# Two-layer state-space and attention trunk: norm chain in three stages, weights' low parts on VectorE, tables behind h, gate row on the load queue

## The chip, the cores and the metric

One core of one Trainium2 chip runs the whole program. The metric is device time in microseconds (us), the median over runs; lower is better. Engine names below are those of the profile: PE is TensorE (PEld its weight loads), DVE VectorE, ACT ScalarE, POOL GpSimd, SP the queue from which nearly all loads are issued.

## The reference, cut to what matters

Two layers (`DEPTH = 2`) over 512 tokens of width 1024, all in float32. Each layer is a mixer and a feed-forward part, each between two RMS norms:

```python
mod = silu(c) @ w_ada[l] + b_ada[l]          # six vectors of 1024: shift, scale, gate for both parts
h = rmsnorm(x, g_pre_mix) * (1 + scale_m) + shift_m
u, q, k, v, f_logit, g_a, g_b = split(h @ w_in)
y_ssm = s5_branch(u, ...)                    # state-space scan per group, then a GLU
y_att = forgetting_attention(q, k, v, f_logit, b_f)
merged = sigmoid(g_a) * (y_ssm @ w_pa) + sigmoid(g_b) * (y_att @ w_pb)
x = x + gate_m * rmsnorm(merged @ w_o, g_post_mix)
h = rmsnorm(x, g_pre_ffn) * (1 + scale_f) + shift_f
y = (silu(h @ w_ffn_gate) * (h @ w_ffn_up)) @ w_ffn_down
x = x + gate_f * rmsnorm(y, g_post_ffn)
```

## The kernel before, in words

**Products in three parts.** A float32 matrix is split into a high part (fp32r, made by an ACT cast, L235) and a low part (the difference, made by a subtraction, L236). Each product is three matmuls on PE: high by high, high by low, low by high. `unit` (L228) loads 512 KB of a weight into a `wraw` buffer from the SP queue (a ring of three, shared with the `aw` loads of the modulation), casts it and subtracts. Pairs go to a ring of three (`wpair`) or to buffers that are kept (`khi`/`klo`, `kept`). Which engine subtracts is told by strings at the end of `trunk`: `LO_F` (first gate and up weights of the FFN), `LO_O` (the output projection), `LO_Q` (the q and k weights of layer 1); "g" is POOL and "v" DVE. All other units use DVE, but for the four first `w_u` units, which use POOL.

**Order of the work.** PE runs in program order. The other engines' queues are ordered by a list scheduler that follows program order and a priority (`high_priority(offset=300)` lifts an instruction). `Weave` counts PE's time in `W.t` from matmul sizes; `run` walks over a list of jobs, prepares loads some 11 us ahead, and between groups of matmuls polls side generators, each of which says with `yield t` after how much PE time it wants to go on. So a `yield` decides where in PE's order, and in program order, the next piece of a side job stands.

**Side generators that matter here.**

- `ada_later` (L197): the modulation vectors `mod`, 512 columns ("half") at a time: four loads `aw`, eight DVE steps over 128x512 into `acc` (L210, L212), matmuls `adap` that sum over partitions, a transpose, `derive`. For layer 0's third to fifth vector with pace 4.0, for the last seven, in layer 0's FFN, with pace 3.6.
- `finish` (L371): after the last row of a half (256 tokens) of a part's output: factors of the output norm (a chain of eleven small DVE steps, L308 and L285 to L301), the new x (L368), its squares on ACT (L386), the factors again, the scaled copy on ACT (L390); then after `WAIT["m"]` four times four transposes `hT` on PE, and `split_h` (L327), which makes high and low part of h (ACT L336, DVE L337 and L338).
- `gate_row` (L316): the row `grow` by which the output is multiplied (L364): a DMA from POOL's queue writes 1024 single values of `modg` to DRAM (L320), a second one reads them back to all partitions (L321).
- `ssm_consts` (L572): tables and matrices of the state-space branch for a quarter of the groups: B, T on POOL, G partly on DVE; PE turns B (`bltp`) and forms `mtp`. Layer 0's are made in its mixer, layer 1's ahead, in layer 0's FFN (`ssm_ahead`, L661), and stored in DRAM.
- `ssm_small` (L483): some two hundred DVE steps over 128x32 at the start, of which `ssm_consts` is built.
- `forget` (L815): the decay of the attention; its matmuls `fp`, then ACT and DVE steps in turn.

**Around the parts.** After the mixer's output projection (`wop`), the FFN's first jobs (`pair_first`, `kept_one`) take h half by half: `gtp` and `upp` into four PSUM buffers, `sil` (L1127) frees `gtp`'s. After the FFN's last products (`dnp`) the next layer's `first4` takes q and k from weights that are kept.

Of the kernel before, what the change touches and what calls it, by code (L numbers as in the profile page):

```python
# [11 lines left out]
F32 = mybir.dt.float32  # L12
# [65 lines left out]
def trunk(tc, a, out, dbg=None):  # L78
# [13 lines left out]
    with contextlib.ExitStack() as ctx:  # L92
# [65 lines left out]

        have = set()

        def derive(l, m, c0, c1):
            sl = mod[:, l, 8 * m + c0:8 * m + c1]

            def gv(at):
                return vec[:, l, at + c0:at + c1]
            if m == 1:
                v.scalar_tensor_tensor(modg[:, l, 0, c0:c1], sl, 1.0, gv(VG1), ALU.add, ALU.mult)
            elif m == 4:
                v.scalar_tensor_tensor(modg[:, l, 2, c0:c1], sl, 1.0, gv(VG3), ALU.add, ALU.mult)
# [27 lines left out]
        def ada_later(ns, pace):  # L197

            for n in ns:
                l, m = divmod(n, 6)  # L200
                for hf in range(2):
                    acc = sp.tile([128, 512], F32, tag="acc", name="acc", bufs=1)
                    for q in range(4):
                        w = wp.tile([128, 1024], F32, tag="wraw", name="aw", bufs=3)
                        nc.sync.dma_start(w, a["w_ada"][n - 2, hf, q])
                        for i in range(2):
                            kt = 2 * q + i
                            wk = w[:, 512 * i:512 * i + 512]
                            if kt == 0:
                                v.tensor_scalar(acc, wk, cond[:, 0:1], None, ALU.mult)  # L210
                            else:
                                v.scalar_tensor_tensor(acc, wk, cond[:, kt:kt + 1], acc, ALU.mult, ALU.add)  # L212
                        yield pace if q < 3 else pace + 2.0
                    p = aps("adap")
# [11 lines left out]


        def unit(src, n=1024, at=None, lo_eng=None, pin=False):  # L228
            raw = wp.tile([128, 1024], F32, tag="wraw", name="wraw", bufs=3)
            nc.sync.dma_start(raw[:, 0:n], src)  # L230
            if at is None:
                w = wp.tile([128, 2, 1024], F32R, tag="wpair", name="wpair", bufs=3)
                at = w[:, 0], w[:, 1]
            hi, lo = (x[:, 0:n] for x in at)
            i = sc.copy(hi, raw[:, 0:n])  # L235
            j = (lo_eng or v).tensor_tensor(lo, raw[:, 0:n], hi.bitcast(F32), ALU.subtract)  # L236
            if pin:
                tc.keep_in_program_order(i)
                tc.keep_in_program_order(j)
            return hi, lo  # L240
# [74 lines left out]

        def gate_row(l, which):  # L316

            gi = 1 if which == 0 else 3
            at = tc.dram_tile([KT, 128], F32, name=f"grow{l}{which}")
            g.dma_start(at.rearrange("k p -> p k"), modg[:, l, gi])  # L320
            g.dma_start(grow, at.rearrange("k p -> (k p)").unsqueeze(0).to_broadcast([128, D]))  # L321

# [48 lines left out]
        def finish(l, which, o, hf, nxt):  # L371
# [8 lines left out]
            with tc.high_priority(offset=300):  # L380
                r = factors(o["s"][hf], 2, 2)
                s2 = sums(2)
                ys = []
                for t in range(2):
                    xs, y = new_x(o, hf, t, r[:, t:t + 1])
                    sc.activation(y, xs, AF.Square, accum_out=s2[:, t:t + 1])  # L386
                r = factors(s2, 2)
                for t in range(2):
                    xs, y = xR[:, 2 * hf + t], o["y"][hf][:, t]
                    sc.activation(y, xs, AF.Copy, scale=r[:, t:t + 1])  # L390
                    ys.append(y)
            yield WAIT["m"][which]
            while not o["free"]:
# [178 lines left out]
        def ssm_consts(l, q):  # L572
# [44 lines left out]
            G = quad([128, 2, 4, 4, 2, 16], name="G")  # L617
            g.memset(G, 0.0)
            pmul(v, cf, lpw, lpn, 3, G[:, 0], G[:, 1], 1)
# [5 lines left out]
            T = quad([128, 2, 4, 128], name="T")  # L625
            g.tensor_copy(T[:, :, :, 0:8], head[:, :, ps4])
            for k in range(4):
                rotate(g, T, [phs[k][i][:, ps4] for i in range(2)], 8 << k, 4)
            yield WAIT["b"][l]
# [12 lines left out]
            M = quad([128, 2, 4, 128], name="M")  # L642
            g.memset(M[:, 0], 0.0)
            p = mps("mtp")
# [10 lines left out]
            sc.copy(M[:, 1], rho4[:, ps4].unsqueeze(2).to_broadcast([128, 4, 128]))  # L655
            g.memset(M[:, 1, :, 0:1], 0.0)
            return (blt, G, T, M), (B.rearrange("p i a b c d -> p i (a b c d)"), C.rearrange("p (i a) -> p i a", i=2))
# [157 lines left out]
        def forget(l, st, fw):  # L815
# [142 lines left out]
        def mix_jobs(l, R, st, done, nxt):  # L958

            def f_job(at):  # L960
                if at == FP[l]:
                    job(3.5, 0, lambda: f_weights(l), lambda fw: forget(l, st, fw))

# [107 lines left out]
            def wo_rows(ws, hf, kts, first=False, last=False):  # L1071

                if first and hf == 0:
                    W.wait(lambda: (l, 2) in have)
                    gate_row(l, 0)
                if first:
# [13 lines left out]
                if last:  # L1090
                    W.add(finish(l, 0, o, hf, nxt), 0.0)

# [17 lines left out]
        def ffn_jobs(l, R, prev, nxt):  # L1110
# [133 lines left out]
            def down(w, ts, dh, i, first, last):  # L1244
                if (dh, first) == (0, True):
                    W.wait(lambda: (l, 5) in have)
                    gate_row(l, 1)
                if first:
# [9 lines left out]
                if last and dh:  # L1258
                    W.add(finish(l, 1, d, ts[0] // 2, nxt), 0.0)

# [15 lines left out]
        def first_jobs(l, R, prev, st):  # L1276
# [31 lines left out]
            for hf in range(2):  # L1308
# [64 lines left out]
        for _ in range(4):  # L1373
            next(smalls, None)
        u_done(st, R, pu)
# [108 lines left out]
```

## Time and profile before

| | |
|---|---|
| median of 3 runs | 1606.41 us (1606.28 to 1606.72) |
| profiled execution | 1615.16 us |
| its span in the profile | 1613.4 us |
| PE busy | 1499.9 us (93%) |
| DVE, ACT, POOL busy | 926.4, 622.9, 342.6 us |
| mean granted PE clock | 0.962 of full speed |
| bytes read from HBM | 193.15 MB |

A row of a timeline has the start in us, the duration in us, the engine, the line of the kernel, the operation, output <- inputs by the program's names, and the count of instructions merged; in brackets stand the engine's idle time before it and what ended it. The granted clock is a share of PE's full 2.4 GHz; 0.5 is its lower level of 1.2 GHz.

### The profile page before, as it was taken

To read this page: it belongs to the slowest core of one execution; us is meant where nothing else is said; L and a number is where in the kernel's file an instruction comes from. 1 tells how busy PE (TensorE), PEld (TensorE's weight loads), DVE (VectorE), ACT (ScalarE), POOL (GpSimd) and SP (SyncE) were. 2 spreads that over 40 slices of the span, in tenths; PEclk is the share of its full clock that TensorE was granted. 3 is DMA by queue.
4 is the path that set the end of the run, shared out by engine and by line. 5 is a ranking of instruction groups with operands and counts; after the bars stand their busy time and mean duration, and the time that the engine had idled before them with its cause. 6 is when DMAs were issued, how large, how long until landed. Compare 5 with 4: busy or idle time off the path is not lost.

```text
span 1613.4 us, 21312 instructions
## 1 busy us (share of the span) xinstructions
PE 1499.9 (93%) x8080; PEld 1250.6 (78%) x8080; DVE 926.4 (57%) x1772; ACT 622.9 (39%) x1103; POOL 342.6 (21%) x460
## 2 busy tenths in 40 slices
PE   7799798999879978999996999999997999999997
PEld 6688676778779756878875998877776988888886
DVE  7828866767745776756567249364656322333344
ACT  3235545554432424323235224465534322332231
POOL 1607714332205664000013000032213000000000
PEclk8899899899989989999998999999997999999999
DMA  8221244554203656776664224232332122322341
GB/s 330 62 90 44 79 135 145 182 170 144 80 26 118 207 185 236 227 185 213 209 170 144 105 81 155 92 105 79 105 105 91 32 74 92 101 95 92 104 144 52
DMA packets 57718, 205.06 MB, mean 127 GB/s; under 512 B 7040, under 2 KB 8192, under 8 KB 56592
## 3 DMA queue, kind: packets, MB, share of 16 engines
q1 hardware_dynamic: 54320, 192.16, 36.8%
q0 software_dynamic: 3008, 10.50, 1.8%
q8 instruction: 63, 1.03, 0.3%
q10 hardware_dynamic: 288, 1.05, 0.2%
q14 instruction: 39, 0.32, 0.1%
HBM read 193.15 MB, written 10.53 MB: 126 GB/s over the span
## 4 chain that ended last, share of the span: by engine, by line
PE 62%; DVE 18%; DMA 9%; ACT 4%; POOL 4%; issue 3%; SPq 0%; ACTq 0%; DVEq 0%; POOLq 0%
PE gtp L85 13%; PE upp L85 13%; PE dnp L85 9%; PE gbp L85 5%; PE qkp L85 5%; PE tokp L85 4%; PE gap L85 3%; DVE wpair L236 3%; DMA aw<-in_w_ada_dram 2%; PE pap L85 2%; DMA wraw<-in_w_down_dram 2%; DMA C<-in_bc_dram 2%; DMA wraw<-in_w_up_dram 1%; PE sps L85 1%; PE ops L85 1%
## 5 line engine op out<-in xcount | busy, mean ns | idle before, releaser
L236 DVE TENSOR_TENSOR wpair<-wraw,wpair 128x1024 fp32r<-128x1024 f32 x188 | 235.9, 1256 | 328.6 <-ACT wpair L235 328.2
L235 ACT CAST wpair<-wraw 128x1024 fp32r<-128x1024 f32 x193 | 201.9, 1047 | 339.2 <-issue 88.0
L85 PE MATMUL gtp<-h,wpair 128*128 128x512 f32 (+1 forms) x912 | 210.3, 387 | 21.0 <-ACT sil L1127 21.0
L85 PE MATMUL upp<-h,wpair 128*128 128x512 f32 (+1 forms) x1008 | 219.8, 370 | 0.0
L85 PE MATMUL dnp<-wpair,act 128*128 128x512 f32 x864 | 208.9, 401 | 8.3 <-ACT wpair L235 4.5
L85 PEld LDWEIGHTS gtp<-h,wpair 128*128 128x128 f32 x912 | 169.8, 196 | 54.4 <-ACT sil L1127 21.4
L85 PEld LDWEIGHTS upp<-h,wpair 128*128 128x128 f32 x1008 | 177.1, 188 | 32.7 <-issue 1.2
L85 PEld LDWEIGHTS dnp<-wpair,act 128*128 128x128 f32 x864 | 166.5, 194 | 45.6 <-ACT wpair L235 4.9
L212 DVE SCALAR_TENSOR_TENSOR acc<-aw,cond,acc 128x512 f32<-128x512 f32 x140 | 110.5, 789 | 69.2 <-DMA aw<-in_w_ada_dram 67.6
L85 PE MATMUL tokp<-wpair,h 128*128 128x512 f32 x384 | 98.6, 413 | 15.5 <-DVE h L338 12.1
L85 PEld LDWEIGHTS tokp<-wpair,h 128*128 128x128 f32 x384 | 82.9, 250 | 26.9 <-DVE h L338 13.7
L85 PE MATMUL gbp<-h,wpair 128*128 128x512 f32 x384 | 97.6, 401 | 0.0
L85 PE MATMUL gap<-h,wpair 128*128 128x512 f32 x384 | 93.3, 398 | 0.0
L1132 DVE TENSOR_TENSOR actf<-sil,upp 128x512 f32<-128x512 f32 (+1 forms) x54 | 31.5, 586 | 92.7 <-PE upp L85 84.4
L85 PEld LDWEIGHTS gbp<-h,wpair 128*128 128x128 f32 x384 | 69.5, 188 | 17.5 <-issue 3.2
L85 PEld LDWEIGHTS gap<-h,wpair 128*128 128x128 f32 x384 | 71.7, 190 | 14.3
L1127 ACT ACTIVATE sil<-gtp 128x512 f32<-128x512 f32 (+1 forms) x54 | 27.8, 518 | 136.8 <-PE gtp L85 136.8
L236 POOL TENSOR_TENSOR klo<-wraw,khi 128x1024 fp32r<-128x1024 f32 x19 | 46.2, 2438 | 161.7 <-PE wop L85 88.9
L893 ACT ACTIVATE sx<-sx,mn 128x512 f32<-128x512 f32 (+3 forms) x64 | 35.5, 557 | 57.6 <-DVE mn L891 57.2
L876 POOL TENSOR_SCALAR_AFFINE_SELECT cb<-cb 128x128 f32<-128x128 f32 x64 | 24.7, 387 | 154.3 <-DVE mn L891 117.9
L85 PE MATMUL qkp<-h,wpair 128*128 128x512 f32 (+1 forms) x240 | 52.5, 371 | 3.9 <-DVE y L356 3.9
L336 ACT ACTIVATE h<-hT,mod,modg 128x256 fp32r<-128x256 f32 (+1 forms) x56 | 32.4, 594 | 50.7 <-PE hT L85 20.9
(293 smaller groups left out, 2553.6 us busy)
## 6 DMA issues: line engine op xcount, KB each, us to landing
aw<-in_w_ada_dram SPq DMA_DIRECT2D x80, 512.0 KB, 4.3
wraw<-in_w_down_dram SPq DMA_DIRECT2D x50, 512.0 KB, 3.6
wraw<-in_w_gate_dram SPq DMA_DIRECT2D x44, 512.0 KB, 3.4
wraw<-in_w_up_dram SPq DMA_DIRECT2D x44, 512.0 KB, 3.4
aw<-in_w_ada_dram SPq DMA_DIRECT2D x8, 1024.0 KB, 16.2
wraw<-in_w_ga_dram SPq DMA_DIRECT2D x16, 512.0 KB, 3.5
wraw<-in_w_gb_dram SPq DMA_DIRECT2D x16, 512.0 KB, 3.4
wraw<-in_w_o_dram SPq DMA_DIRECT2D x16, 512.0 KB, 3.3
```

What stands on the lines that cost most here:

```text
L85: te.matmul(o, lhsT, rhs, **kw)
L212: v.scalar_tensor_tensor(acc, wk, cond[:, kt:kt + 1], acc, ALU.mult, ALU.add)
L235: i = sc.copy(hi, raw[:, 0:n])
L236: j = (lo_eng or v).tensor_tensor(lo, raw[:, 0:n], hi.bitcast(F32), ALU.subtract)
L336: ic = sc.activation(hi[:, i], ps[i], AF.Identity, scale=by, bias=to)
L876: g.affine_select(out=cb[e][:, n - 128:n], in_=cb[e][:, n - 128:n], compare_op=ALU.is_ge, fill=1e30, base=0, pattern=[[-1, 128]], channel_ ...
L893: sc.activation(sx[:, e, 0:n], sx[:, e, 0:n], AF.Exp, scale=-1.0, bias=mn, accum_out=rs)
L1127: sc.activation(t, pa[:, cs], AF.Silu)
L1132: v.tensor_tensor(t2, t, pb[:, cs], ALU.mult)
```

## The change

Eight edits, made together:

1. `finish` is cut into three stages with a `yield` between them, and starts 1.0 later: factors and new x; 4.0 later the squares and second factors; 5.0 later the scaled copies; 2.5 later the transposes. Before, all DVE and ACT steps stood in one place and the transposes 11.0 (mixer) or 11.5 (FFN) later.
2. `LO_F`, `LO_O` and `LO_Q` are all "v".
3. In `ssm_consts` the POOL steps run on DVE for layer 1 (those ahead); layer 0's stay on POOL.
4. The steps of `ssm_small` are put behind the last DVE step of the first h in DVE's order.
5. `derive` writes a gate's values to DRAM as soon as they are made (still from POOL's queue); `gate_row` only reads them, from the SP queue, behind the latest weight load.
6. `ada_later` waits 6.0 longer, not 2.0, before a half's matmuls.
7. `forget` becomes a side generator: its first three steps get priority, and the rest comes 6.0 later.
8. `load` holds the latest load, for edit 5.

```diff
@@ derive
+                if m in (2, 5):
+                    at = gates[l, m // 5] = tc.dram_tile([KT, 128], F32, name=f"gate{l}{m}")
+                    g.dma_start(at.rearrange("k p -> p k"), modg[:, l, m - 1 if m == 2 else 3])
@@ ada_later
-                        yield pace if q < 3 else pace + 2.0
+                        yield pace if q < 3 else pace + 6.0
@@ unit
-            nc.sync.dma_start(raw[:, 0:n], src)
+            load[:] = [nc.sync.dma_start(raw[:, 0:n], src).ins]
@@ gate_row
-            g.dma_start(at.rearrange("k p -> p k"), modg[:, l, gi])
-            g.dma_start(grow, at.rearrange("k p -> (k p)").unsqueeze(0).to_broadcast([128, D]))
+            with tc.issue_after(behind):
+                nc.sync.dma_start(grow, gates[l, which].rearrange("k p -> (k p)").unsqueeze(0).to_broadcast([128, D]))
@@ finish
                 r = factors(o["s"][hf], 2, 2)
+                ys = [new_x(o, hf, t, r[:, t:t + 1])[1] for t in range(2)]
+            yield WAIT["m"][0]
+            with tc.high_priority(offset=300):
                 s2 = sums(2)
                 for t in range(2):
-                    xs, y = new_x(o, hf, t, r[:, t:t + 1])
-                    sc.activation(y, xs, AF.Square, accum_out=s2[:, t:t + 1])
+                    sc.activation(ys[t], xR[:, 2 * hf + t], AF.Square, accum_out=s2[:, t:t + 1])
                 r = factors(s2, 2)
+            yield WAIT["m"][1]
+            with tc.high_priority(offset=300):
                 for t in range(2):
-                    sc.activation(y, xs, AF.Copy, scale=r[:, t:t + 1])
-            yield WAIT["m"][which]
+                    sc.activation(ys[t], xR[:, 2 * hf + t], AF.Copy, scale=r[:, t:t + 1])
+            yield WAIT["m"][2]
@@ ssm_consts (and so for every g. of it: memsets of B, G, M, the copy and rotations of T)
-            g.memset(B, 0.0)
-            pmul(g, bc[:, 0:2], lpd, lpd, 4, B[:, 0], B[:, 1], 0)
+            e = v if l else g
+            e.memset(B, 0.0)
+            pmul(e, bc[:, 0:2], lpd, lpd, 4, B[:, 0], B[:, 1], 0)
@@ forget
-            sc.activation(fb, p[32:40, :], AF.Identity, bias=vec[32:40, l, VBF:VBF + 1])
-            v.tensor_tensor(fa, p[0:8, :], fb, ALU.add)
-            v.scalar_tensor_tensor(fb, fa, -1.0, fa, ALU.mult, ALU.max)
+            with tc.high_priority(offset=300):
+                (the same three)
+            yield 6.0
             sc.activation(fb, fb, AF.Exp, scale=-1.0)
@@ mix_jobs, wo_rows, down
-                    job(3.5, 0, lambda: f_weights(l), lambda fw: forget(l, st, fw))
+                    job(3.5, 0, lambda: f_weights(l), lambda fw: W.add(forget(l, st, fw)))
-                    gate_row(l, 0)
+                    gate_row(l, 0, load[0])
-                    W.add(finish(l, 0, o, hf, nxt), 0.0)
+                    W.add(finish(l, 0, o, hf, nxt), 1.0)
@@ trunk
-        LO_F = ["gv", "gv", "gg", "gg", "vv"]
-        LO_O = "vgvgvvvg"
-        LO_Q = "gggggggg"
+        LO_F = ["vv"] * 5
+        LO_O = "v" * 8
+        LO_Q = "v" * 8
-                "z": (5.0, 6.0), "s": (4.2, 4.2), "t": (5.0, 5.6), "o": (2.6, 2.6), "m": (11.0, 11.5),
+                "z": (5.0, 6.0), "s": (4.2, 4.2), "t": (5.0, 5.6), "o": (2.6, 2.6), "m": (4.0, 5.0, 2.5),
-                split_h(0, 0, hs, hT, q, ALL)
+                ins, _ = split_h(0, 0, hs, hT, q, ALL)
         for _ in range(4):
-            next(smalls, None)
+            with tc.issue_after(ins):
+                next(smalls, None)
```

## Rows read from the trace of the kernel before

**Rows 1.** What PE waited for over the whole execution: line waited for, us in total, times, longest us. The three longest.

```profile
PE gtp L85 <- ACT sil L1127: 21.0, 2, 10.9
PE hT L85 <- ACT y L390: 16.0, 7, 9.2
PE tokp L85 <- DVE h L338: 12.1, 3, 8.8
```

**Rows 2.** Timeline of the start: three `tokp` groups of PE, then DVE's first step (L337) for the last quarter of h and one of the last table steps.

```profile
26.95 1.24 PE L85 MATMUL tokp<-wpair,h 128*128 128x512 f32 x2 [2.40 <-ACT h L336]
42.96 5.56 PE L85 MATMUL tokp<-wpair,h 128*128 128x512 f32 x22 [2.35 <-DVE h L338]
69.04 6.85 PE L85 MATMUL tokp<-wpair,h 128*128 128x512 f32 x22 [8.77 <-DVE h L338]
...
66.65 1.51 DVE L337 TENSOR_SCALAR hw<-hT,modg,mod 128x512 f32<-128x512 f32 x2
72.53 0.18 DVE L557 COPY ph<-bank 128x32 f32<-128x32 f32 x1
```

**Rows 3.** Timeline around layer 0's `fp`: ACT, then PE (the first of its rows from the quarter before).

```profile
168.59 0.63 ACT L826 ACTIVATE fb<-fb 8x512 f32<-8x512 f32 x1 [7.97 <-DVE fb L825]
170.54 0.60 ACT L736 ACTIVATE M<-yp 128x512 f32<-128x512 f32 x1
...
139.02 0.66 PE L85 MATMUL bltp<-ident,B 128*128 128x128 f32 x4 [1.58 <-ACT M L736]
171.19 1.11 PE L85 MATMUL bltp<-ident,B 128*128 128x128 f32 x4 [9.46 <-ACT M L736]
171.95 2.85 PE L85 MATMUL gap<-h,wpair 128*128 128x512 f32 x6
```

**Rows 4.** Timeline around the first gate row: POOL, DVE, PE.

```profile
265.80 1.12 POOL L320 DMA_DIRECT2D grow<-modg  x1 [3.30 <-DVE ah L277]
280.87 0.75 DVE L212 SCALAR_TENSOR_TENSOR acc<-aw,cond,acc 128x512 f32<-128x512 f32 x1 [10.33 <-DMA aw<-in_w_ada_dram]
280.90 0.58 POOL L321 DMA_DIRECT2D grow<-grow  x1 [12.32 <-DMA grow<-modg]
282.13 1.22 DVE L236 TENSOR_TENSOR wpair<-wraw,wpair 128x1024 fp32r<-128x1024 f32 x1
282.27 1.12 PE L85 MATMUL tps<-ident,sx 128*128 128x128 f32 x4 [4.97 <-POOL sx L895]
285.31 0.78 PE L85 MATMUL pap<-yh,wpair 128*128 128x512 f32 x1
```

**Rows 5.** The transition from layer 0's mixer to its FFN, second half of the tokens: DVE, POOL, ACT, PE.

```profile
437.89 2.33 DVE L291 TENSOR_SCALAR nyi<-nm 128x2 int32<-128x2 int32 x1
442.61 0.16 DVE L294 TENSOR_TENSOR nt<-nyi 128x2 f32<-128x2 f32 x1
448.68 2.33 DVE L296 SCALAR_TENSOR_TENSOR nu<-nt 128x2 f32<-128x2 f32 x1
...
433.05 7.15 POOL L236 TENSOR_TENSOR klo<-wraw,khi 128x1024 fp32r<-128x1024 f32 x3 [44.02 <-PE wop L85]
...
451.89 2.19 ACT L390 ACTIVATE y<-xR,ny 128x1024 f32<-128x1024 f32 x2 [3.31 <-DVE ny L300]
454.10 1.28 ACT L1127 ACT_TABLE_LOAD   x1
455.39 0.66 ACT L1127 ACTIVATE sil<-gtp 128x256 f32<-128x256 f32 x2
...
455.83 2.93 PE L85 MATMUL gtp<-h,wpair 128*128 128x256 f32 x12 [10.08 <-ACT sil L1127]
462.04 1.68 PE L85 MATMUL upp<-h,wpair 128*128 128x256 f32 x12
```

**Rows 6.** The same transition in layer 1: one DVE step of the chain.

```profile
1228.83 5.34 DVE L291 TENSOR_SCALAR nyi<-nm 128x2 int32<-128x2 int32 x1
```

**Rows 7.** Busy time of the engines by stretch (start:end, length, PE, PEld, DVE, ACT, POOL with instruction counts, granted PE clock, DMA share, GB/s): the ahead-built quarters, then the transition from the FFN to the next mixer.

```profile
542.00:625.00 83.00, 67.97 (x339) 52.18 (x339) 59.66 (x89) 25.85 (x58) 60.14 (x87) 0.90 0.65 212
833.00:880.00 47.00, 32.73 (x157) 27.39 (x157) 35.97 (x62) 21.38 (x33) 20.36 (x9) 0.85 0.47 145
```

**Rows 8.** DVE groups by line from 542 to 625 us (busy us, mean ns | idle before, releaser), then the same first line from 640 to 800 us, where POOL is idle.

```profile
L212 DVE SCALAR_TENSOR_TENSOR acc<-aw,cond,acc 128x512 f32<-128x512 f32 x22 | 20.5, 932 | 14.0 <-DMA aw<-in_w_ada_dram 13.8
L610 DVE COPY C<-C 64x128 f32<-64x128 f32 x4 | 6.1, 1528 | 6.0 <-DMA C<-in_bc_dram 5.9
...
L212 DVE SCALAR_TENSOR_TENSOR acc<-aw,cond,acc 128x512 f32<-128x512 f32 x59 | 44.2, 750 | 27.8 <-DMA aw<-in_w_ada_dram 27.1
```

**Rows 9.** DVE steps of the start over the shapes that POOL works on in the ahead-built quarters.

```profile
46.31 0.41 DVE L568 TENSOR_TENSOR rt<-head,bank 128x256 f32<-128x256 f32 x1
122.77 0.67 DVE L702 TENSOR_TENSOR C<-sp,T 128x512 f32<-128x512 f32 x1
```

**Rows 10.** The transition from the FFN to the next mixer: the last transfer of `modg`, DVE, PE.

```profile
823.06 0.90 POOL L320 DMA_DIRECT2D grow<-modg  x1 [119.17 <-DVE modg L173]
867.62 4.91 DVE L338 TENSOR_TENSOR h<-hw,h 128x256 fp32r<-128x256 f32 x2
855.28 0.48 PE L85 MATMUL hT<-ident,y 128*128 128x128 f32 x1 [9.16 <-ACT y L390]
873.28 0.94 PE L85 MATMUL qkp<-h,wpair 128*128 128x256 f32 x6 [3.94 <-DVE y L356]
```

More of the change, by code (lines that the diff above doesn't have):

```diff
@@ L155, in trunk @@
         v.tensor_scalar(vec[:, :, VG1:VG4 + 8], vec[:, :, VG1:VG4 + 8], NF, None, ALU.mult)
-        have = set()
+        have, gates = set(), {}
         def derive(l, m, c0, c1):
@@ L225, in ada_later @@
                     derive(l, m, c0, c1)
+        load = []
         def unit(src, n=1024, at=None, lo_eng=None, pin=False):
             raw = wp.tile([128, 1024], F32, tag="wraw", name="wraw", bufs=3)
-            nc.sync.dma_start(raw[:, 0:n], src)
+            load[:] = [nc.sync.dma_start(raw[:, 0:n], src).ins]
             if at is None:
@@ L314, in sums, with gate_row @@
             return sp.tile([128, n], F32, tag="sums", name="sums", bufs=4)
-        def gate_row(l, which):
-            gi = 1 if which == 0 else 3
-            at = tc.dram_tile([KT, 128], F32, name=f"grow{l}{which}")
-            g.dma_start(at.rearrange("k p -> p k"), modg[:, l, gi])
-            g.dma_start(grow, at.rearrange("k p -> (k p)").unsqueeze(0).to_broadcast([128, D]))
+        def gate_row(l, which, behind):
+            with tc.issue_after(behind):
+                nc.sync.dma_start(grow, gates[l, which].rearrange("k p -> (k p)").unsqueeze(0).to_broadcast([128, D]))
         def new_h(r):
@@ L381, in finish @@
                 r = factors(o["s"][hf], 2, 2)
+                ys = [new_x(o, hf, t, r[:, t:t + 1])[1] for t in range(2)]
+            yield WAIT["m"][0]
+            with tc.high_priority(offset=300):
                 s2 = sums(2)
-                ys = []
                 for t in range(2):
-                    xs, y = new_x(o, hf, t, r[:, t:t + 1])
-                    sc.activation(y, xs, AF.Square, accum_out=s2[:, t:t + 1])
+                    sc.activation(ys[t], xR[:, 2 * hf + t], AF.Square, accum_out=s2[:, t:t + 1])
                 r = factors(s2, 2)
+            yield WAIT["m"][1]
+            with tc.high_priority(offset=300):
                 for t in range(2):
-                    xs, y = xR[:, 2 * hf + t], o["y"][hf][:, t]
-                    sc.activation(y, xs, AF.Copy, scale=r[:, t:t + 1])
-                    ys.append(y)
-            yield WAIT["m"][which]
+                    sc.activation(ys[t], xR[:, 2 * hf + t], AF.Copy, scale=r[:, t:t + 1])
+            yield WAIT["m"][2]
             while not o["free"]:
@@ L617, in ssm_consts @@
             G = quad([128, 2, 4, 4, 2, 16], name="G")
-            g.memset(G, 0.0)
+            e.memset(G, 0.0)
             pmul(v, cf, lpw, lpn, 3, G[:, 0], G[:, 1], 1)
@@ L625, in ssm_consts @@
             T = quad([128, 2, 4, 128], name="T")
-            g.tensor_copy(T[:, :, :, 0:8], head[:, :, ps4])
+            e.tensor_copy(T[:, :, :, 0:8], head[:, :, ps4])
             for k in range(4):
-                rotate(g, T, [phs[k][i][:, ps4] for i in range(2)], 8 << k, 4)
+                rotate(e, T, [phs[k][i][:, ps4] for i in range(2)], 8 << k, 4)
             yield WAIT["b"][l]
@@ L642, in ssm_consts @@
             M = quad([128, 2, 4, 128], name="M")
-            g.memset(M[:, 0], 0.0)
+            e.memset(M[:, 0], 0.0)
             p = mps("mtp")
@@ L655, in ssm_consts @@
             sc.copy(M[:, 1], rho4[:, ps4].unsqueeze(2).to_broadcast([128, 4, 128]))
-            g.memset(M[:, 1, :, 0:1], 0.0)
+            e.memset(M[:, 1, :, 0:1], 0.0)
             return (blt, G, T, M), (B.rearrange("p i a b c d -> p i (a b c d)"), C.rearrange("p (i a) -> p i a", i=2))
@@ L822, in forget @@
             fa, fb, fc = (tmp([8, 512], name=n) for n in ("fa", "fb", "fc"))
-            sc.activation(fb, p[32:40, :], AF.Identity, bias=vec[32:40, l, VBF:VBF + 1])
-            v.tensor_tensor(fa, p[0:8, :], fb, ALU.add)
-            v.scalar_tensor_tensor(fb, fa, -1.0, fa, ALU.mult, ALU.max)
+            with tc.high_priority(offset=300):
+                sc.activation(fb, p[32:40, :], AF.Identity, bias=vec[32:40, l, VBF:VBF + 1])
+                v.tensor_tensor(fa, p[0:8, :], fb, ALU.add)
+                v.scalar_tensor_tensor(fb, fa, -1.0, fa, ALU.mult, ALU.max)
+            yield 6.0
             sc.activation(fb, fb, AF.Exp, scale=-1.0)
@@ L1246, in down @@
                     W.wait(lambda: (l, 5) in have)
-                    gate_row(l, 1)
+                    gate_row(l, 1, load[0])
                 if first:
@@ L1258, in down @@
                 if last and dh:
-                    W.add(finish(l, 1, d, ts[0] // 2, nxt), 0.0)
+                    W.add(finish(l, 1, d, ts[0] // 2, nxt), 1.0)
             for i in range(4, 11):
```

## The prediction

> **What bounds the kernel now.** The page comes first: PE is busy 1499.9 of 1613.4 us, so at most 113 us are idle, and the row of the granted clock shows slices under 1, each where PE had idled (0.90 and 0.85 in two such stretches [rows 7]). Then PE's list of waits, which says on whom it idles [rows 1]: on an ACT step before the FFN (`sil`), on the scaled copy of the norm chain (`hT`), on h at the start. Last the timeline at each place, to see what ended late. Nearly all stalls stand in six places, and PE is dense between them, so what the change does is worth what it does there.
>
> **VectorE and POOL hold each other up.** While POOL forms low parts (433.05 to 440.20), a DVE step over 128x2 takes 2.33 us; the next, without POOL, 0.16 [rows 5]. In layer 1 one such step takes 5.34 [rows 6], and a step of h 4.91 for two [rows 10]. In the ahead-built stretch POOL is busy 60.14 of 83 us [rows 7], and a DVE step of the modulation takes 932 ns, against 750 where POOL is idle [rows 8]. So a low part of 1.22 us that moves to DVE [rows 4] replaces a POOL step of 7.15/3 = 2.4 [rows 5] that could hold DVE for as long.
>
> **The change part by part.** The sum is made against the profiled execution (1615.16, span 1613.4) and taken from the median, 1606.4, which is 8.8 lower.
>
> *Tables behind h.* DVE takes up the last quarter of h at 66.65, though PE, past its transposes, had waited since 60.3 (69.04 less 8.77); the tables run until 72.53 [rows 2]. With DVE free, h needs the chain L337, L338, some 2.3 us for the first half (half of 1.51, plus one step of 0.67 [rows 9], plus queueing); of the stalls 8.77, 2.40 and 2.35 [rows 2] I keep 2, 0 and 1.1, and gain 10.4. PE's 22 matmuls then take 5.56 rather than 6.85: 1.3 more. On the other side the some two hundred small steps now run while the first q units are due; their low parts must find room between them. What is late is at worst one low part behind some 8 us of tables; I charge 1, keep 4 to 14, and take 11. POOL's first matrices start later, hidden by the wait of 25 before them; without that cover up to 8 is lost, which is in the low end.
>
> *Forget.* ACT idles 7.97 for DVE between two of its steps; the Gelu behind them starts at 170.54 and PE waits 9.46 for the PSUM buffer; a quarter before, the same wait was 1.58 [rows 3]. With the rest 6.0 later the Gelu passes. 7.9 is saved, and 1.7 that PE lost at its lower level, 1.2 GHz, after that idle time (1.11 against 0.66, and six matmuls in 2.85, where 22 in 5.56 [rows 2] give 1.5): 9.5 (5 to 11).
>
> *Gate row.* In the first transfer POOL stands 12.32 us for its own write, and the softmax step that PE wants (`sx`) behind it; PE idles 4.97 [rows 4]. After, POOL does not wait. But the write itself, 1024 single values, is still there, and what it does to other transfers with it: DVE waits 10.33 for an `aw` load that lands with the write, and forms the next weight's low part only at 282.13, done at 283.35. PE then gets on at about 283.4, not at 286.4 (its third matmul from 285.31 on): 3, and some 2 of slow clock: 5 (0 to 10, the upper being both stalls there and their slow stretch). The read moves from POOL's queue to SP's: it stands behind a load already issued, its data have long been written, and `grow`'s last reader is hundreds of us back, so SP does not wait. It costs one more 512 KB among the loads, hidden while the ring is full.
> On the rule side: the Trainium skill's page "DMA: Bandwidth & Descriptors", section "Issuing engines are not separate DMA queues", says that transfers from all queues run on the same engines and another issuer only saves issue time. By it this part would be worth POOL's issue alone, 0.6, and the sum 4 less; the 12.32 of waiting on POOL speaks for more, the 10.33 on DVE for the rule.
>
> *Norm chain and low parts, mixer to FFN, twice.* `sil` stands behind the scaled copies on ACT (454.10 behind 451.89), and these behind the chain, of which three steps of 2.33 or 2.32 are over by 6.5; in layer 1 the two steps are over by 5.2 and 2.2 [rows 5, 6]. After, DVE forms the low parts itself (five of 1.22 around the chain, of which two may get in its way), and by the new places the copies stand about where `sil` does. PE cannot do without `sil`'s table load and step, about 2 us. So of 10.08 and 10.92 (the total of 21.0 in [rows 1]) 7 and 8 go, with 2 each of slow clock (12 matmuls in 2.93 against 1.68, more than once [rows 5]). For the first half, the transposes stand 2.5 later in PE's order, so that the waits on `y` (16.0 in all [rows 1] less 9.2 in the third transition [rows 10], 3.4 each) go, and with them some 1.5 of slow clock: 4.5 each, I take 4.5 and 4. Together 13.5 and 15: 28.5 (13 to 32; the low end is the chain still late by half).
> Whether `sil` pays more: its load takes 1.28 and it starts within 0.01 after [rows 5]. The Trainium skill, "ScalarE: Activation LUTs", section "What ACT_TABLE_LOAD costs", has a drain of 1.38 us beside it; by that the rest of each wait would be 1.4 longer and the sum 2.8 less. The trace shows no such time, and I go by it.
>
> *Ahead-built matrices on DVE.* For a quarter: eight products of B at 0.41; the rotations of T, whose largest four steps are about 0.67, 0.67, 0.41, 0.41 and the rest some 3.3 together; memsets and a copy, up to 2.9 (the sizes priced by [rows 9]): 11 us, 44 in all. DVE is busy 59.66 of 83 us there with nearly three quarters [rows 7]: adding 33, taking off what POOL inflates (22 x 0.18 = 4, four copies at 1.53 for about 0.2 = 5, some 5 in other steps [rows 8]) and 5 for the slower modulation leaves 74 of the 68 that PE needs. So DVE is the limit there: the 15 us that PE idles cannot all go, and a chunk of some 16 us, with up to 6 of waiting for its load (L610), may outlast the pairs in the ring (two units of 5.4 ahead). I take -3, between +10 (waits on `acc` and POOL gone) and -20 (each quarter 5 more).
>
> *Slower modulation.* Its fourteen halves take some 4 us longer each, 56 in all by PE's work. The last ended just before 823, and the transition's first transposes were due at 846 (855.28 less 9.16) [rows 10]: now it runs through that transition.
>
> *FFN to mixer.* PE idles 9.16 and 3.94 there [rows 10], both behind a DVE that POOL holds up. After, DVE's 35.97 of 47 us [rows 7] lose some 13 of inflation, but get eight low parts (10) and two halves of modulation (14): no room for a gain on that count. For it, the last single-value write, which at 823 held the loads up ahead of this stage, moves behind. I take +2 (-10 to +12).
>
> Sum: 11 + 9.5 + 5 + 28.5 - 3 + 2 = 53. 1606.4 - 53 = 1553.4. Low ends: 4 + 5 + 0 + 13 - 20 - 10 = -8, so 1614; high ends: 14 + 11 + 10 + 32 + 10 + 12 = 89, so 1517.
>
> **The rivals.**
> - *All clears.* DVE keeps up in the ahead-built quarters (+10) and the next transition (+12): 53 + 13 + 10 = 76, 1530. For it: much of DVE's load there is inflation. Against: the 74 of 68 above.
> - *VectorE becomes the bound* there: -20 and -10, so 53 - 17 - 12 = 24, 1582. For it: the same count; DVE is in order and already waits for loads of C and `aw` [rows 8].
> - *The chain's wait moves*: the copies still stand ahead of `sil`, and the low parts fill DVE instead of POOL: half of 28.5 goes, 39, 1567.
> - *Slower*: in the four ahead-built quarters each chunk holds up the weights' low parts by 14 us more than the ring covers (4 x 14 = 56 less on a term of -3 and a sum of 53): 1609 and over. It decides from the point where no low part gets in between a quarter's steps for 24 us; the chunk with its load wait is 22. Against: units prepared before a quarter stand ahead of it in program order.
> - *It doesn't do what it says*: the scheduler places the chain and tables as before; 1606, which the removed POOL steps make unlikely.
>
> **How the numbers follow.** Forecast (1537 to 1570, the sum with the two VectorE terms at half their bounds) 0.50; all clears 0.15; VectorE the bound 0.20; the chain's wait moves 0.07; no change 0.03; slower 0.05. Faster by over 0.2%, about what a measurement of this kernel can tell from none, 0.92; same 0.03; slower 0.05. The range leaves out the slower case, the unchanged one and the outer part of the second rival: 1515 to 1592.
>
> **What would show it.** Right: chain steps of 0.2 us everywhere; PE's gaps before `gtp` at 2 to 3 us; the last `tokp` group within 2 us of h's transposes; a `bltp` wait under 2 beside `fp`; POOL idle in layer 0's FFN but for its stores; DVE still waiting some 10 us beside each single-value write. Wrong: PE waiting on `wpair` from DVE between 500 and 600, or on h in the transition to layer 1, by more than 20 us in all; or q units waiting for low parts behind the tables.

## The result: 1558.1 us, and the profile of the changed kernel

The changed kernel takes 1558.13 us (median of 4 runs, 1556.75 to 1559.68) beside 1606.35 for the kernel before: a ratio of 0.9705, 95% interval 0.9688 to 0.9723, 48 us less. Run again on another chip it gave 0.9668 (0.9645 to 0.9691). So the medians of the same kernel differ by some 6 us between these two chips, and an edit worth less than that can only be told from a run beside it on the same chip, or from its place in the trace.

The page after: span, engines, granted clock.

```profile
span 1556.7 us, 21254 instructions
PE 1487.2 (96%) x8080; PEld 1241.5 (80%) x8080; DVE 921.3 (59%) x1914; ACT 622.0 (40%) x1103; POOL 195.9 (13%) x314
PEclk9999899999999989999998999999999999999999
```

What PE waits for after (in total, times, longest us), to set against [rows 1].

```profile
PE bltp L85 <- ACT M L741: 10.7, 3, 8.2
PE adap L85 <- DVE acc L215: 8.1, 2, 4.7
PE hT L85 <- ACT y L395: 7.9, 4, 5.9
...
PE tokp L85 <- DVE h L341: 1.8, 1, 1.8
...
PE gtp L85 <- ACT sil L1134: 1.6, 2, 1.2
```

`gtp` on `sil` fell from 21.0 us to 1.6, `tokp` on h from 12.1 to 1.8, `hT` on `y` from 16.0 to 7.9. At the top now stands the Gelu beside `fp`, which the forget edit was to remove.

Where the 56.7 us between the two profiled executions went, from the start of the same PE instruction in both traces (us; the kernel before ran 8.8 over its median in its own, so some 8 of these gains belong to that one execution, and the table cannot tell where):

| From the mark above to the start of ... | before | after | gained |
|---|---|---|---|
| first `utp` | 77.11 | 62.42 | 14.7 |
| layer 0's `fp` | 154.82 | 146.61 | -6.5 |
| first `glup` | 231.04 | 222.15 | 0.7 |
| 100th `gbp` | 321.43 | 305.66 | 6.9 |
| first `gtp` (FFN, layer 0) | 433.66 | 416.27 | 1.6 |
| first ahead-built `bltp` (33rd) | 526.62 | 498.65 | 10.6 |
| 457th `gtp`, after the ahead-built quarters | 681.90 | 644.43 | 9.5 |
| 430th `dnp` | 830.33 | 792.63 | 0.2 |
| 193rd `tokp` (layer 1) | 921.98 | 884.76 | -0.5 |
| 193rd `wop` | 1171.46 | 1134.46 | -0.2 |
| 650th `gtp` (FFN, layer 1) | 1224.72 | 1180.03 | 7.7 |
| 864th `dnp` | 1558.95 | 1502.07 | 12.2 |

The transition that [rows 5] show, now: the chain on DVE with low parts between its steps, ACT, PE.

```profile
419.37 0.17 DVE L297 TENSOR_SCALAR nyi<-nyi 128x2 int32<-128x2 int32 x1
419.44 1.23 DVE L241 TENSOR_TENSOR klo<-wraw,khi 128x1024 fp32r<-128x1024 f32 x1
420.57 0.16 DVE L299 TENSOR_TENSOR nt<-nyi 128x2 f32<-128x2 f32 x1
...
428.57 1.28 ACT L1134 ACT_TABLE_LOAD   x1
429.87 0.38 ACT L1134 ACTIVATE sil<-gtp 128x256 f32<-128x256 f32 x1
430.62 2.19 ACT L395 ACTIVATE y<-xR,ny 128x1024 f32<-128x1024 f32 x2 [0.38 <-DVE ny L305]
...
430.30 3.14 PE L85 MATMUL gtp<-h,wpair 128*128 128x256 f32 x24 [1.17 <-ACT sil L1134]
```

Every step of the chain takes 0.15 to 0.17 us. The trace has 108 such steps over 128x2 (`nyi`, `nt`, `nu`, `ny`), and none is over 0.2; of the 108 of the kernel before, six are, 2.32 to 5.34. `sil` now stands ahead of the scaled copies on ACT, and PE waits 1.17 where it waited 10.08.

### The profile page after: what moved, and what is told of

The parts are those of the page before. It is cut to its first block, busy times and chain, and to the rows that moved or that the text cites. A ratio compares the mean times of both kernels' runs of the same rounds, so it can differ in the third digit from the quotient of the medians.

```text
span 1556.7 us, 21254 instructions
## 1 busy us (share of the span) xinstructions
PE 1487.2 (96%) x8080; PEld 1241.5 (80%) x8080; DVE 921.3 (59%) x1914; ACT 622.0 (40%) x1103; POOL 195.9 (13%) x314
## 4 chain that ended last, share of the span: by engine, by line
PE 72%; DVE 13%; DMA 8%; ACT 3%; issue 2%; POOL 2%; SPq 0%; DVEq 0%; ACTq 0%; POOLq 0%
PE upp L85 14%; PE gtp L85 13%; PE dnp L85 8%; PE gbp L85 6%; PE gap L85 6%; PE wop L85 5%; PE tokp L85 4%; DMA aw<-in_w_ada_dram 3%; PE pap L85 2%; DVE wpair L241 2%; PE qkp L85 2%; DMA wraw<-in_w_down_dram 2%; PE pbp L85 2%; PE glup L85 1%; PE sps L85 1%
## 5 line engine op out<-in xcount | busy, mean ns | idle before, releaser
L85 PE MATMUL upp<-h,wpair 128*128 128x512 f32 (+1 forms) x1008 | 223.6, 374 | 2.1 <-DVE wpair L241 2.0
L85 PE MATMUL dnp<-wpair,act 128*128 128x512 f32 x864 | 204.4, 395 | 1.9 <-DVE wpair L241 1.9
L85 PE MATMUL gtp<-h,wpair 128*128 128x512 f32 (+1 forms) x912 | 203.1, 378 | 1.6 <-ACT sil L1134 1.6
L85 PEld LDWEIGHTS dnp<-wpair,act 128*128 128x128 f32 x864 | 163.1, 190 | 37.3 <-DVE wpair L241 2.6
L85 PEld LDWEIGHTS gtp<-h,wpair 128*128 128x128 f32 x912 | 164.8, 188 | 33.9 <-ACT sil L1134 2.0
L215 DVE SCALAR_TENSOR_TENSOR acc<-aw,cond,acc 128x512 f32<-128x512 f32 x140 | 106.2, 758 | 49.2 <-DMA aw<-in_w_ada_dram 47.7
L85 PE MATMUL wop<-kept,mg 128*128 128x512 f32 x192 | 48.7, 395 | 2.3 <-DVE mg L1067 2.3
L902 POOL TENSOR_SCALAR sx<-sx,rr 128x512 f32<-128x512 f32 (+3 forms) x64 | 45.6, 722 | 29.1 <-DVE rr L901 26.2
L85 PEld LDWEIGHTS qkp<-h,wpair 128*128 128x128 f32 x240 | 41.9, 189 | 8.6 <-DVE wpair L241 1.5
```

What stands on the lines that cost most here:

```text
L85: te.matmul(o, lhsT, rhs, **kw)
L902: g.tensor_scalar(sx[:, e, 0:n], sx[:, e, 0:n], rr, 0.0, ALU.mult, ALU.add)
```

## The experiments

Each is the changed kernel with one thing undone or added, unless it says otherwise. Ratios are to the kernel before on the same chip. The first four ran on one chip, the next four on a second, the last four on a third.

**1. Low parts back on POOL.**

```
-        LO_F, LO_O, LO_Q = ["vv"] * 5, "v" * 8, "v" * 8
+        LO_F, LO_O, LO_Q = ["gv", "gv", "gg", "gg", "vv"], "vgvgvvvg", "gggggggg"
```

> The changed kernel with the low parts of FFN, output projection and q/k weights back on POOL (edit 2 undone); all else as changed. Theory POOL: the transitions were late because POOL's low parts hold DVE's chain; then steps of 2.3 us come back there, PE's waits before gtp too, and the time is 1578 to 1588 (20 to 30 above 1558). Rival PLACES: it was the new places of the chain's stages that let sil pass; then the time stays within 6 of 1558, steps of 2.3 us or not.

Measured: 1592.0 us, 0.9889 (0.9861 to 0.9918): 30 to 35 of the changed kernel's 48 us are gone, by its two ratios. Its first transition: POOL, the chain on DVE, PE; then PE in layer 1.

```profile
428.26 2.38 POOL L241 TENSOR_TENSOR kept<-wraw,kept 128x1024 fp32r<-128x1024 f32 x1
436.95 2.35 POOL L241 TENSOR_TENSOR kept<-wraw,kept 128x1024 fp32r<-128x1024 f32 x1 [6.32 <-PE gtp L85]
...
428.36 2.30 DVE L296 TENSOR_SCALAR nyi<-nm 128x2 int32<-128x2 int32 x1
436.98 2.35 DVE L301 SCALAR_TENSOR_TENSOR nu<-nt 128x2 f32<-128x2 f32 x1
439.36 0.16 DVE L302 SCALAR_TENSOR_TENSOR ny<-nu,nyi 128x2 f32<-128x2 f32 x1
...
444.14 3.14 PE L85 MATMUL gtp<-h,wpair 128*128 128x256 f32 x13 [6.48 <-ACT sil L1134]
...
1227.40 4.80 PE L85 MATMUL gtp<-h,wpair 128*128 128x256 f32 x21 [7.88 <-ACT sil L1134]
```

A step over 128x2 that starts with a POOL low part (436.95, 436.98) ends with it, 2.35 us for 0.16, and the waits for `sil` are back although the chain is staged.

**2. The norm chain in one part again** (one `yield WAIT["m"][which]` of 11.0 or 11.5 behind the whole chain, and no start put off by 1.0, as in the kernel before).

> The changed kernel with the norm chain in one stage as before, transposes 11.0 and 11.5 later (edit 1 undone). Theory POOL: low parts were the cause, so only the transposes that stand too early cost, 2 to 4 us a transition: 1562 to 1570. Rival PLACES: most of the transitions' gain goes, 1578 or more, with PE waiting on sil behind the copies again.

Measured: 1569.18, 0.9749 (0.9723 to 0.9775): 7 to 13 us worse, by the changed kernel's two ratios. Not before the FFN, where PE waits 1.24 for `sil`, but at the change to layer 1 (PE):

```profile
819.57 0.47 PE L85 MATMUL hT<-ident,y 128*128 128x128 f32 x1 [8.78 <-ACT y L393]
854.21 0.48 PE L85 MATMUL hT<-ident,y 128*128 128x128 f32 x1 [6.18 <-ACT y L393]
```

The changed kernel waits 5.88 and 0.80 at these two (7.19 and 0.80 when run again), and from the 430th `dnp` to the 193rd `tokp` it is 6.5 shorter (92.1 for 98.6).

**3. The ahead-built matrices back on POOL.**

```
-            e = v if l else g
+            e = g
```

> The changed kernel with layer 1's state-space matrices ahead on POOL again (edit 3 undone). By the forecast this edit was worth -3 (-20 to +10): the time would be 1548 to 1561, with DVE less busy in that stage. Rival: the stage ran 9.5 us shorter after the change, and this edit is why: 1565 to 1570, with DVE steps of over 900 ns there again.

Measured: 1555.89, 0.9669 (0.9639 to 0.9698): between nothing and 6 us better than with the edit. Stretch 514 to 597 us, in which nearly three quarters stand as in [rows 7], the changed kernel and then this one (columns as there):

```profile
514.00:597.00 83.00, 71.87 (x367) 56.16 (x366) 64.75 (x168) 33.27 (x79) 7.29 (x13) 0.94 0.74 219
```

```profile
514.00:597.00 83.00, 73.10 (x372) 57.23 (x371) 64.23 (x93) 34.32 (x80) 60.03 (x88) 0.96 0.76 227
```

DVE is busy for nearly the same time in either form, though it has 75 steps less here: POOL held it up for about as long as the moved work takes. A modulation step of 743 ns takes 931 in this run (533 to 616 us).

**4. The tables free again** (no tie behind h).

> The changed kernel without the tie of the tables behind h (edit 4 undone). PE reached the first utp 14.7 us sooner after the change, but lost 6.5 of it up to fp. Theory GIVEN BACK: the later tables cause that loss, so undoing costs 8: 1564 to 1568. Rival: the loss between is something else and stays: 1570 to 1574.

Measured: 1567.7, 0.9745 (0.9713 to 0.9777): 6 to 12 us worse. PE at the start of this kernel, then in the q units of the changed one:

```profile
71.48 7.45 PE L85 MATMUL tokp<-wpair,h 128*128 128x512 f32 x22 [8.77 <-DVE h L341]
80.14 0.60 PE L85 MATMUL utp<-ident,un 128*128 128x128 f32 x4
```

```profile
102.69 1.20 PE L85 MATMUL qkp<-h,wpair 128*128 128x512 f32 x4 [1.06 <-DVE wpair L241]
116.87 9.25 PE L85 MATMUL tokp<-wpair,h 128*128 128x512 f32 x33 [3.37 <-ACT k L810]
```

The tie brings the first `utp` 17.7 us forward (62.42 for 80.14). From there to `fp` the changed kernel takes 84.2 us (146.61 - 62.42) and this one 77.7 (157.85 - 80.14), so 6.5 is given back; 11.2 stays. Of the 6.5, 5.1 stand at the wait of 3.37 and in the slow clock behind it (0.62 from 116.8 to 121): the same 42 `tokp` take 14.66 from 111.30 in the changed kernel, and 9.52 from 127.67 here. What ends last there is POOL, whose first matrices wait for tables and come late; `fw` is cleared on POOL behind them, and ACT, which needs it, stands in front of the copy of k. POOL and ACT in the changed kernel, then ACT here:

```profile
103.10 2.01 POOL L571 TENSOR_TENSOR rt<-T,ph 128x512 f32<-128x512 f32 x1 [2.10 <-DVE ph L562]
109.88 0.95 POOL L845 MEMSET fw<- 128x1024 f32 x1
...
110.86 0.25 ACT L846 CAST fw<-fraw 128x64 fp32r<-128x64 f32 x1 [4.85 <-POOL M L661]
116.23 0.58 ACT L810 COPY k<-qkp 128x512 f32<-128x512 f32 x1
```

```profile
122.78 0.24 ACT L846 CAST fw<-fraw 128x64 fp32r<-128x64 f32 x1 [0.39 <-POOL fw L845]
```

**5. The Gelu put ahead of exp by force** (`with tc.issue_after(st["gelu"]):` around the exp and Ln of the forget row).

> The changed kernel with one thing added: the forget chain's exp and Ln are tied behind the Gelu that stands ready beside them, so that ScalarE runs the Gelu first. In the changed kernel TensorE still waits 8.23 us for that Gelu (154.20 to 162.43 of its span), because exp stands ahead of it and waits 7.41 us for VectorE's fb. Theory 'the order on ScalarE was not changed': that wait falls to about 1.6 us (the Gelu itself and its hand-over), the later layer's place of the same kind changes little, and the time falls by 6 to 8 us against the changed kernel: 0.966 of the kernel before. Rival 'VectorE is late anyway': the wait only moves to the first instruction that needs the forget row, and the time stays at 0.9705.

Measured: 1555.06, 0.9691 (0.9669 to 0.9713): no difference that the two chips' ratios allow to tell. First the changed kernel, DVE and ACT beside `fp`; then this one, ACT and PE.

```profile
155.16 3.20 DVE L241 TENSOR_TENSOR wpair<-wraw,wpair 128x1024 fp32r<-128x1024 f32 x2
158.28 0.67 DVE L830 TENSOR_TENSOR fa<-fp,fb 8x512 f32<-8x512 f32 x1
...
159.84 0.63 ACT L833 ACTIVATE fb<-fb 8x512 f32<-8x512 f32 x1 [7.41 <-DVE fb L831]
161.78 0.60 ACT L741 ACTIVATE M<-yp 128x512 f32<-128x512 f32 x1
```

```profile
152.45 0.60 ACT L741 ACTIVATE M<-yp 128x512 f32<-128x512 f32 x1 [2.72 <-PE yp L85]
159.41 0.63 ACT L834 ACTIVATE fb<-fb 8x512 f32<-8x512 f32 x1 [4.58 <-DVE fb L831]
159.94 0.56 ACT L642 COPY blt<-bltp 128x512 f32<-128x512 f32 x1
...
160.56 2.08 PE L85 MATMUL sp<-U,blt 128*128 128x128 f32 x8 [3.74 <-ACT blt L642]
```

The 8.23 us wait is gone, but exp, still waiting for DVE, now holds up the next ACT copy (`blt`). PE waits 3.74 there, and from `bltp` (152.20) to the first `glup` (223.70) this kernel takes 71.5 us, the changed one 68.6 (153.60 to 222.15): worse at the place itself.

**6. The gate row written in 128-byte runs** (`modg` is also cleared once at the start, which the cut leaves out).

```
-                    g.dma_start(at.rearrange("k p -> p k"), modg[:, l, m - 1 if m == 2 else 3])
+                    gi = m - 1 if m == 2 else 3
+                    gt = tmp([128, 32], name="gt")
+                    v.transpose(gt, modg[:, l].rearrange("p a b -> p (a b)"))
+                    for b in range(4):
+                        g.dma_start(at[:, 32 * b:32 * b + 32], gt[32 * b + 8 * gi:32 * b + 8 * gi + 8, :])
```

> The changed kernel with one thing changed: the 1024 single values of each gate row are turned in 32x32 blocks on VectorE and leave in four writes of 8 runs of 128 bytes, instead of one write of 1024 runs of 4 bytes. The change moved that write to an earlier place (270.8, 552.2, 700.4 and 862.0 us), it did not take it away. Theory 'the single-value write is a cost that moved': the waits of over 10 us that other loads show beside each write go, the PE waits adap<-acc beside 552.2 and 862.0 (4.7 and 4.4 us) shrink, and the time falls by 3 to 8 us: 0.966 to 0.968. Rival 'hidden where it now stands': 0.9705 within 2 us.

Measured: 1542.98, 0.9616 (0.9593 to 0.9639): 8 to 14 us better than the changed kernel, more than expected. Ten us beside layer 0's second write, the changed kernel (write issued at 552.21) and then this one (551.45; the stretch from 553.24, as far behind the issue as the first, has 302 GB/s):

```profile
554.00:564.00 10.00, 10.00 (x46) 8.27 (x45) 3.15 (x7) 5.14 (x17) 1.15 (x3) 1.00 1.11 101
```

```profile
551.00:561.00 10.00, 10.00 (x45) 8.26 (x45) 7.82 (x17) 5.31 (x18) 3.60 (x7) 1.00 0.93 324
```

The DMA engines are taken in both, but move 101 GB/s beside the single values and 324 without them. What that holds up in the changed kernel, DVE and then PE, and the granted clock around that wait (last column but two), beside that of this kernel:

```profile
566.28 0.43 DVE L597 TENSOR_TENSOR pm<-C,lpd 128x256 f32<-128x256 f32 x1 [8.92 <-DMA C<-in_bc_dram]
580.03 0.65 PE L85 MATMUL adap<-acc,ones 128*32 128x128 f32 x8 [4.74 <-DVE acc L215]
...
575.00:590.00 15.00, 9.84 (x57) 6.83 (x56) 13.82 (x38) 6.20 (x11) 1.60 (x3) 0.77 0.71 244
```

```profile
569.00:584.00 15.00, 13.88 (x84) 10.86 (x84) 12.08 (x27) 8.47 (x23) 1.07 (x2) 1.00 0.87 284
```

A load of C is late by 8.92, DVE stands behind it, PE waits 4.74 for a modulation sum, and the mean clock of these 15 us is 0.77. Here no wait in that stage behind the write is over 1.12, and the clock is 1.00. From the 33rd `bltp` to the 457th `gtp` it takes 138.6 us, the changed kernel 145.8 and, run again, 145.5: some 7 of the gain stand at this one write.

**7. The gate row written and read on POOL's queue at first use, as before.**

> The changed kernel with the edit of the gate row undone: the write and the read of the row stand again on POOL's queue, at the first use. Theory of the prediction (5 us, bounds 0 to 10): the time rises by about 5 us against the changed kernel, 0.9736 of the kernel before, most of it in the first layer's first half (the gap at the glup/gbp tiles). Rival 'the other loads wait in either place': the same 4-byte runs hold up loads at the use instead of ahead of it, and the time rises by under 1.5 us.

Measured: 1561.02, 0.9729 (0.9705 to 0.9754): 4 to 10 us worse by the changed kernel's two ratios; its interval overlaps with the first of theirs and lies above the second. The waits for `sx` that the edit was to take away are 1.41 and 1.01 here, and 0.44 at most in the changed kernel. But the place as a whole did not answer: from the first `glup` to the 100th `gbp` it takes 85.1 us (306.71 - 221.58), and the changed kernel 83.5 and, run again, 85.6.

**8. The wait in the modulation's halves set back** (`pace + 6.0` to `pace + 2.0`).

> The changed kernel with the wait between the last products of an ada column and its matmuls set back from the pace plus 6 to the pace plus 2. Theory 'the ahead-built stage got shorter from the pace': the waits adap<-acc (8.1 us in 2) grow, the stage from 470 to 620 us loses 3 to 7 us, and the time rises by that much less what the later ada work gives back in FFN to mixer: 0.971 to 0.974. Rival 'the pace only moves the work': within 1.5 us of the changed kernel.

Measured: 1551.43, 0.9666 (0.9642 to 0.9689): 0 to 6 us better. It moves work between stages: from the 33rd `bltp` to the 457th `gtp` 153.0 us (the changed kernel 145.8), but from the 430th `dnp` to the 193rd `tokp` 82.7 (92.1). That is 7.2 lost, 9.4 won.

**9. The changed kernel again.**

> The changed kernel itself, on the same chip as the next three, so that they are compared side by side: 0.9705 of the kernel before, within its interval (0.969 to 0.972).

Measured: 1551.98, 0.9668 (0.9645 to 0.9691). It is the partner for the next three. In the traces of the two, the stage from the 457th `gtp` to the 430th `dnp` takes 148.2 and 144.3: a stage of one kernel can differ by some 4 us.

**10. The forget edit undone** (one part, no priority).

> The changed kernel with the edit of the forget row undone: the whole chain in one part again, its first three instructions no longer ahead of the rest. The prediction gave this edit 9.5 us (5 to 11). The trace of the changed kernel still has the wait that it was to take away (8.23 us for the Gelu, 9.46 before), so the theory now is: the edit is worth the 1.2 us by which that wait got shorter, and no more than 3 us in all; the time rises by 0 to 3 us against the changed kernel. Rival 'the edit works elsewhere, in the later layer or by the order that follows': it rises by 5 us or more.

Measured: 1553.11, 0.9681 (0.9657 to 0.9704): 1.1 us worse than its partner, whose runs (1550.0 to 1553.8) overlap with its own (1552.5 to 1557.5). The edit is worth about nothing; the wait for the Gelu is 7.29 here and 6.87 in the partner.

**11. The kernel before with the low parts on VectorE alone.**

> The kernel before with one edit alone: the low parts of the weights all on VectorE, nothing else. Undoing this edit in the changed kernel cost 34 us. Theory 'the low parts carry the change by themselves': the waits gtp<-sil of 10.08 and 10.92 us fall below 4 us each and the time falls by 20 to 30 us, 0.982 to 0.988. Rival 'they only pay with the chain staged': the chain of the norm then queues behind low parts on VectorE, the waits stay over 6 us each, and the time falls by less than 12 us.

Measured: 1569.2, 0.9773 (0.975 to 0.9796): 35.6 of its partner's 52.8 us, beyond what was expected. PE before the FFN in both layers, with the chain still in one part:

```profile
438.37 1.69 PE L85 MATMUL gtp<-h,wpair 128*128 128x256 f32 x12 [1.16 <-ACT sil L1127]
...
1204.47 1.70 PE L85 MATMUL gtp<-h,wpair 128*128 128x256 f32 x12 [2.31 <-ACT sil L1127]
```

**12. Runs of 128 bytes, the short wait, and the ahead-built matrices on POOL together.**

> The changed kernel with three things: the gate row written in 128-byte runs (alone 0.9616), the pace set back to plus 2 (alone 0.9666) and the ahead-built matrices back on POOL (alone 0.9669). If the three work at places of their own, the sum of the ratios gives 0.9616 - 0.0039 - 0.0036 = 0.954 of the kernel before. If they share the place (all three touch the ahead-built stage from 500 to 640 us, where the wait for an ada sum goes), it is 0.959 to 0.962.

Measured: 1533.4, 0.9555 (0.9534 to 0.9577): 18.6 us faster than the changed kernel beside it, and the fastest form run. The sum of the three alone, 0.954, lies in its interval: they work at places of their own. Where the changed kernel waited 5.88 for `y` (7.19 in the partner) at the change to layer 1, PE now waits 0.35, with no modulation step left in that stretch and the clock at 1.00:

```profile
797.27 0.33 PE L85 MATMUL hT<-ident,y 128*128 128x128 f32 x1 [0.35 <-ACT y L400]
...
788.00:835.00 47.00, 41.62 (x287) 37.61 (x286) 36.84 (x88) 28.14 (x47) 0.00 (x0) 1.00 0.37 124
```

## Why the prediction was right, and where it was not

1553.4 was forecast and 1558.1 measured, 1552.0 on another chip; the profiled execution fell by 56.6 where the sum said 53. Of the rivals none came: DVE did not become the bound, the chain's wait did not move, and not everything cleared. But that the sum holds is partly luck, because two wrong terms cancel.

- **Mixer to FFN, 28.5 forecast.** From the 100th `gbp` to the first ahead-built `bltp` the gain is 12.2 (13.5 forecast), in layer 1 19.9 (15; by its own terms, 8, 2 and 4, it would be 14, and the forecast 1554.4): 32.1. The mechanism, a DVE step that lasts as long as POOL's, is shown by runs 1 and 11. What was not seen is that the low parts need no help there: alone they give 33.5 at the same marks. With the chain short, `sil` passes the scaled copies even where the chain is one part. The staging earns its 7 to 13 chiefly at another place, the change to layer 1 (run 2), where the prediction gave it nothing. On `sil` the trace decides between the two readings: it starts 0.02 behind its table load (428.57 and 1.28, 429.87), so the drain in the Trainium skill's "ScalarE: Activation LUTs", section "What ACT_TABLE_LOAD costs", is not seen here either.
- **Tables, 11 (4 to 14).** 14.7 came at the start and 6.5 went back before `fp`: 8.2; by run 4 it is 17.7 less 6.5, 11.2. The step was right; its two sides were both too small. 11.7 (10.4 and 1.3) was forecast where 14.7 to 17.7 came. The charge of 1 for the low parts behind the tables fits (PE waits 1.06 for one), but POOL's first matrices, which the sum left out as "hidden by the wait of 25 before them" (its low end allowed for them), were not hidden: 5.1 of the 6.5 stand behind them, by way of ACT (run 4).
- **Forget, 9.5 (5 to 11).** This failed. "With the rest 6.0 later the Gelu passes": it did not, and the edit brought about 1 (run 10). In the changed kernel's trace ACT still has exp ahead of the Gelu (159.84, 161.78), and the wait is 8.23. The fault lies deeper than the order: run 5 makes the Gelu pass and gains nothing, because exp then holds up `blt` instead. What is late is VectorE. `fb` leaves ACT at 151.1 (150.44 and 0.68), and DVE takes up `fa` at 158.28, behind the G matrix and two low parts. The kernel before has the same order, `fa` at 167.04 behind two low parts from 163.92 on, so the priority did not bring `fa` forward. The prediction asked where the Gelu would go, and not what stood next behind exp.
- **Gate row, 5 (0 to 10).** The total fits (4 to 10 by run 7), the place only in part: the waits of 1.41 and 1.01 for `sx` go. The 6.9 gained around the first row is not shown to be this edit's: with the edit undone 5.3 of it stay (90.4 before, 85.1), and the low parts alone give 3.0. What run 7 loses shows most at the change to layer 1, where PE waits 4.35 for q, and 2.15 or 2.12 with the edit; how much of the total stands there stays open. The prediction did say that the write stays and holds up other loads. It left out its price: run 6 puts 8 to 14 us on it. That is more than the edit.
- **Ahead-built on DVE, -3 (-20 to +10).** The stage gained 9.5. Not by this edit: run 3 without it keeps 10.6 (144.7 from the 33rd `bltp` to the 457th `gtp`). The slower modulation is worth 7.2 there (run 8; without it PE waits 9.16 for one sum), the low parts alone 3.6 (run 11): between them the whole. The price of the moved work was right, 44 forecast and 45.3 measured (116 steps of run 3's POOL between 450 and 645 us, on DVE in the changed kernel). The bound of 74 us of DVE work in 68 of PE was far off: DVE was busy 64.8 of 83 where PE was 71.9. For nearly three quarters the term added 33 and took off 14 for what POOL inflates; run 3's 64.2 shows that what DVE lost to POOL's hold was nearly as long as the work it took over.
- **FFN to mixer, +2 (-10 to +12).** -0.5, and the working held: the modulation moves into that stage. Sixteen of its DVE steps, the two halves forecast, start there in both traces of the changed kernel and none in the kernel before, and without the slower pace the stage is 9.4 shorter.

So in the ahead-built stage the sum missed 12.5 that the pace and the low parts brought, and lost 8.4 on the forget row that never came. Of the signs named ahead, the chain's 0.16 us, `gtp`'s gaps (1.2 where 2 to 3 were expected), the last `tokp` group (0.98 and 1.76) and an idle POOL in layer 0's FFN came out. DVE's wait for a load beside a single-value write came at two of the four (8.92 and 12.26; 4.56 at the first). A `bltp` wait under 2 did not come, and one of the signs of being wrong did in part: a q unit waits 1.06 for a low part behind the tables (run 4).

The Trainium skill, "DMA: Bandwidth & Descriptors", section "Issuing engines are not separate DMA queues", says that transfers of all queues share the engines, and that another issuer saves issue time alone. At the first row it has the better of the argument, since to move the issue changed nothing there that two executions can tell (run 7); and run 6 shows the sharing itself, 101 GB/s against 324.

## What to carry to other kernels

When a VectorE step over a few columns takes 2 us where its like takes 0.16, look for a POOL step that starts with it: even where nothing waits for POOL, its step costs what the held VectorE step holds up, and work that moves from POOL to VectorE may cost VectorE next to nothing. Before an edit that lets one instruction pass another, ask what stands behind the one that is passed; if its own input is late, the wait only moves on by one. A tiny transfer of single values is priced by the loads beside it. Moving it to an earlier place left 8 to 14 us of that price here; writing it in longer runs took them away.

## What the runs showed of the hardware that was not expected

- One write of 4 KB in 1024 single values takes 13.0 us from issue to landing in layer 0's FFN, and for ten of them all DMA engines together move 101 GB/s. The same 4 KB as four writes of 128-byte runs land in 5.0 us each, with 324 GB/s beside them (the changed kernel, then run 6):

```profile
gate<-modg POOLq DMA_DIRECT2D x1, 4.0 KB, 13.0
```

```profile
gate<-gt POOLq DMA_DIRECT2D x4, 1.0 KB, 5.0
```

- The single pause of 4.74 from 575.29 on (shown with run 6) is followed by a stretch at the lower of PE's two levels, 1.2 GHz, with 1.00 again from 585 on (the changed kernel; granted clock in the last column but two). Run 6, which has neither this pause nor this stretch, is 7.2 shorter in that stage. So the pause costs some 7 us, not 4.74:

```profile
578.00:584.00 6.00, 3.55 (x18) 1.94 (x20) 5.93 (x17) 2.10 (x4) 0.00 (x0) 0.50 0.84 258
585.00:600.00 15.00, 15.00 (x68) 12.38 (x67) 10.21 (x19) 8.27 (x21) 1.29 (x3) 1.00 0.79 277
```

- A VectorE step over 128x2 that meets a POOL low part ends when POOL's does: 2.35 us for both in run 1, where the next takes 0.16. In the traces of the kernel before and of run 1, 23 steps over 128x2 start within a low part, and each ends within 0.25 us of its end. The Trainium skill, "SBUF — State Buffer", section "SBUF: two separate sides", calls the port pair that the two engines share an exclusive lock, held for the whole instruction and not shared out, where a VectorE step has two SBUF inputs or runs in a two-port mode. The rows agree for the step of two inputs (436.98). Not every VectorE step is held: one that reads a PSUM tile (`wop`) takes 0.68 beside the low parts of [rows 5], as it does without them (0.69 at 417.70 in the changed kernel):

```profile
433.13 0.68 DVE L364 TENSOR_TENSOR y<-wop,grow 128x512 f32<-128x512 f32 x1
```
